# Pool groups by running sums and one difference, and attention units in four turns

## The chip, the core and the metric

The kernel runs on one core of a Trainium2 chip. The metric is device time in microseconds (us), the median of several executions of the whole kernel. Five engines work side by side, each with its own list of instructions in a fixed order: PE multiplies matrices and transposes by a multiplication with the identity, DVE does elementwise work with one or two inputs, ACT applies functions and copies, POOL does small elementwise work, and SP issues nearly all transfers. An engine takes its list strictly in order and stops at an instruction whose inputs are not there or whose output buffer is still being read.

## The reference

One decoder block over 2048 positions of 1024 values. The input is normed, projected to 2048 columns (512 for a pooling mixer and 512 each for q, k, v of 8 heads), mixed, projected back, and followed by a feed-forward part with 4096 inner columns and a squared relu.

```python
for g, w in enumerate(POOL_WINDOWS):            # 2, 4, 8, 16
    xg = ug[:, :, g, :].astype(jnp.float32)
    cs = jnp.cumsum(xg, axis=1)
    cs_lag = jnp.pad(cs, ((0, 0), (w, 0), (0, 0)))[:, :S]
    count = jnp.minimum(pos + 1, w).astype(jnp.float32)[None, :, None]
    mean = (cs - cs_lag) / count
    outs.append(mean - xg)
pooled = jnp.stack(outs, axis=2)
mapped = jnp.einsum('bsgc,gcd->bsgd', pooled, pool_w.astype(jnp.float32))
...
log1m = jnp.where(mask, jax.nn.log_sigmoid(-z), 0.0)
tail = lax.cumsum(log1m, axis=3, reverse=True) - log1m
log_a = jax.nn.log_sigmoid(z) + tail
a = jnp.where(mask, jnp.exp(log_a), 0.0)
ob = jnp.einsum('bhqk,bhkd->bhqd', a, vb.astype(jnp.float32))
```

So each of four groups of 128 pool channels takes the mean of its last 2, 4, 8 or 16 positions, less the position itself, and maps it with a 128x128 matrix. The attention weight of a key is its sigmoid times the product of one minus the sigmoids of all later keys.

## The kernel before

The 2048 positions are four tiles (j = 0 to 3) of 512. Data lies with channels on the 128 partitions and positions along the row. All large products are made of three multiplications: each fp32 operand is split into a rounded part (ACT, L145) and the rest (DVE, L146), and high times high, high times low and low times high are added up in PSUM (lines 177 to 179).

In the front part (about the first 560 us) PE runs the dense input projection, 24 multiplications of 128x512 for each block of 128 output columns (pd). Between them stand three kinds of narrow work.

- **Pool groups** (`pool_group`, one for each tile and window). ACT brings the projection from PSUM to u, 15 carried positions of the tile before stand ahead of it (POOL copies them with L390 and L395). DVE doubles the window by adding the tile to itself, shifted by 1, 2, 4, 8 (L400: one add for window 2, four for window 16), and L403 scales and subtracts u. ACT and DVE split the result (pls), and PE maps it (L410 to L412, tile pp).
- **Attention units** (`near_unit`, 64 in all: 4 tiles, 8 heads, two pairs of 128 queries each). A unit has stages, and each stage runs in a turn: first the logits on PE (pz), two sigmoids on ACT (sh, sg), a mask on POOL (L661), a running product on DVE (L663, pc) and a product that gives the weights (L672, sg); in its next turn four transposes on PE (L677, pta) and the split of the result (at); in its third turn the products with v (L689, po). `turn_stages` adds a unit and gives each unit in flight its next stage, and keeps two for the next turn. pta has two PSUM buffers, so the transposes of a unit also wait until the split of the unit before the last has read its buffer.
- **Loads** of q, k and v of a head (`near`), which SP issues while the head before is worked on.

The rest (output projection, and the feed-forward part, from about 650 us) is not touched by the change.

A scheduler puts the instructions of all engines in order when the program is built, with a timing model of its own. So an edit also moves instructions that it does not name. On the chip the lists are fixed.

Of the kernel before, what the change touches and what calls it, by code (L numbers as in the profile page):

```python
# [8 lines left out]
F32 = mybir.dt.float32  # L9
# [4 lines left out]
ALU = mybir.AluOpType  # L14

P = 128
S = 2048
D = 1024
T = 512
NT = S // T  # L20
# [8 lines left out]
WARM = 9  # L29
SCRATCH = 2048  # L30
WINDOWS = (2, 4, 8, 16)
PAD = 15
EPS = 1e-6
RATIO_FRONT = (0.3, 0.4, 0.15, 0.4, 0.4, 0.3)
RATIO_TAIL = 0.6
# [10 lines left out]
def hymba_block(ctx: ExitStack, tc: tile.TileContext, xT, gains, w_in, pool_w, w_out, w_up, w_down, out):  # L46
    nc = tc.nc
# [3 lines left out]
    const = pool("const", 1)  # L51
# [55 lines left out]
    for n in (D, D // 2):  # L107
        inv[n] = const.tile([P, 1], F32, name=f"inv{n}")
        nc.vector.memset(inv[n], 1.0 / n)
    recip = const.tile([P, PAD], F32, name="recip")  # L110
    for i in range(PAD):
        nc.vector.memset(recip[:, i:i + 1], 1.0 / (i + 1))
# [9 lines left out]
    yrlast = const.tile([P, 2, 2, TB], F32R, name="yrlast")  # L122
    carry = const.tile([P, len(WINDOWS), PAD], F32, name="carry")
    nc.vector.memset(carry, 0.0)


    qs = [[dram.tile([P, T], F32R, name=f"qs{h}_{j}") for j in range(NT)] for h in range(H)]
    ks = [[dram.tile([P, T], F32R, name=f"ks{h}_{j}") for j in range(NT)] for h in range(H)]
# [13 lines left out]
    def split(dst, src):  # L142

        hi, lo = dst
        nc.scalar.activation(hi, src, AF.Copy)  # L145
        return nc.vector.tensor_tensor(lo, src, hi.bitcast(F32), ALU.subtract)  # L146
# [147 lines left out]
    def pool_weights():  # L294
        raw = pa.tile([P, PAD + T], F32, tag="s", name="pw_raw")[:, 0:4 * P].rearrange("p (g c) -> p g c", g=4)
        nc.sync.dma_start(raw, pool_w)
        pw.append(pa.tile([P, 2, 4, P], F32R, name="pw", bufs=1))
        split((pw[0][:, 0], pw[0][:, 1]), raw)

# [85 lines left out]
    def pool_group(j, g, ps):  # L385
        w = WINDOWS[g]
        if g == 0:
            st[j]["y"] = pa.tile([P, 4, T], F32, tag="yb", name="yb", bufs=1)
        u = pa.tile([P, PAD + T], F32, tag="u", name="u")
        nc.gpsimd.tensor_copy(u[:, 0:PAD], carry[:, g])  # L390
        if j == 0:
            took = nc.vector.tensor_tensor(u[:, PAD:], ps, st[0]["r"], ALU.mult)
        else:
            took = nc.scalar.activation(u[:, PAD:], ps, AF.Copy)
        nc.gpsimd.tensor_copy(carry[:, g], u[:, T:T + PAD])  # L395
        cur, lag = u, 1
        while lag < w:
            nxt = pa.tile([P, PAD + T], F32, tag="s", name="s")
            lo = 2 * lag - 1
            nc.vector.tensor_tensor(nxt[:, lo:], cur[:, lo:], cur[:, lo - lag:PAD + T - lag], ALU.add)  # L400
            cur, lag = nxt, 2 * lag
        pl = pa.tile([P, T], F32, tag="ev", name="pl")
        nc.vector.scalar_tensor_tensor(pl, cur[:, PAD:], 1.0 / w, u[:, PAD:], op0=ALU.mult, op1=ALU.subtract)  # L403
        if j == 0:
            nc.vector.tensor_tensor(pl[:, 0:w - 1], cur[:, PAD:PAD + w - 1], recip[:, 0:w - 1], ALU.mult)
            nc.vector.tensor_tensor(pl[:, 0:w - 1], pl[:, 0:w - 1], u[:, PAD:PAD + w - 1], ALU.subtract)
        d = pa.tile([P, 2, T], F32R, tag="st", name="pls", align_bytes=256, bufs=3)
        split((d[:, 0], d[:, 1]), pl)
        pp = psx.tile([P, T], F32, tag="px", name="pp")
        nc.tensor.matmul(pp, pw[0][:, 0, g], d[:, 0], start=True, stop=False)  # L410
        nc.tensor.matmul(pp, pw[0][:, 0, g], d[:, 1], start=False, stop=False)
        nc.tensor.matmul(pp, pw[0][:, 1, g], d[:, 0], start=False, stop=True)  # L412
        nc.scalar.activation(st[j]["y"][:, g], pp, AF.Copy, scale=gs[:, g:g + 1])
        return took
# [83 lines left out]
    def attend(j, h2):  # L498
        begun[j] = begun.get(j, 0) + 1
        end = begun[j] == H // 2  # L500
        note(lambda: todo.extend([near(j, h2)] + [near_end(j)] * end))
# [131 lines left out]
    def sigmoids(pz):  # L633
        n = pz.shape[-1]
        sh = att.tile([P, T], F32, tag="sh", name="sh")
        nc.scalar.activation(sh[:, T - n:], pz, AF.Sigmoid, scale=-0.125)
        sg = att.tile([P, T], F32, tag="sg", name="sg", bufs=3)
        nc.scalar.activation(sg[:, T - n:], pz, AF.Sigmoid, scale=0.125)
        return sh, sg

# [9 lines left out]
    def near_unit(j, h, p, t):  # L650


        c0 = P if j == 0 and p == 0 else 0
        pz = psz.tile([P, T], F32, tag="pz", name="pz")
        pc = att.tile([P, T + 4], F32, tag="pc", name="pc")
        for i in range(2):
            b, lo = 2 * p + i, c0 if i == 0 else 0
            logits(pz[:, i * 256 + lo:(i + 1) * 256], t["qa"], t["qb"], b, t["kw"][:, b * P + lo:(b + 2) * P], i == 0, i == 1)
        sh, sg = sigmoids(pz[:, c0:])
        own = sg.rearrange("p (i n) -> p i n", i=2)[:, :, P:]  # L660
        nc.gpsimd.affine_select(out=own, in_=own, pattern=[[0, 2], [-1, P]], base=0,  # L661
                                channel_multiplier=1, compare_op=ALU.is_gt, fill=0.0)
        nc.vector.tensor_tensor_scan(pc[:, c0:T][:, ::-1], sh[:, c0:][:, ::-1], later_keys[:, c0:][:, ::-1], 1.0,  # L663
                                     op0=ALU.mult, op1=ALU.max)

        if c0:
            for lo, hi in ((c0, 255), (256, 511)):
                nc.vector.tensor_tensor(sg[:, lo:hi], sg[:, lo:hi], pc[:, lo + 1:hi + 1], ALU.mult)
        else:
            sg2 = sg.rearrange("p (i n) -> p i n", i=2)  # L670
            pc2 = pc[:, 0:T].rearrange("p (i n) -> p i n", i=2)
            nc.vector.tensor_tensor(sg2[:, :, 0:255], sg2[:, :, 0:255], pc2[:, :, 1:256], ALU.mult)  # L672
            nc.gpsimd.tensor_copy(left[j][:, 2 * p:2 * p + 2, h], pc2[:, :, 0])
        yield
        pt = pst.tile([P, T], F32, tag="pt", name="pta")
        for x in range(c0 // P, TB):
            nc.tensor.transpose(pt[:, x * P:(x + 1) * P], sg[:, x * P:(x + 1) * P], ident)  # L677
        at = att.tile([P, 2, T], F32R, tag="at", name="at")
        split((at[:, 0, c0:], at[:, 1, c0:]), pt[:, c0:])
        yield  # L680
        if p == 0:
            t["po"] = pso.tile([P, T], F32, tag="po", name="po")
        po, vw = t["po"], t["vw"]
        both, own, prev = (P, 3 * P, 1, 0), (3 * P, T, 2, P), (0, P, 0, 0)
        av = [(both, 0), (own, 0), (own, 1), (both, 1)] + ([] if c0 else [(prev, 0), (prev, 1)])

        for n, ((lo, hi, v, to), x) in enumerate(av):
            m = DH if x else P
            nc.tensor.matmul(po[0:m, p * 256 + to:p * 256 + to + hi - lo], vw[:, 2 * p + v, 0:m], at[:, x, lo:hi],  # L689
                             start=(p == 0 and n == 0), skip_group_check=True, stop=(p == 1 and n == len(av) - 1))  # L690
        if p == 1:
            if h % 2 == 0:
                t["ot"] = ots[j, h // 2] = att.tile([P, T], F32, tag="ot", name="ot", bufs=1)
            halves_sum(ots[j, h // 2], po, h % 2)
            if h % 2:
                nc.sync.dma_start(os_[j][h // 2], ots.pop((j, h // 2)))
        yield

    ots, stages = {}, []

    def turn_stages():

        for unit in stages:
            next(unit)
        del stages[:len(stages) - 2]

    def near(j, h2):
        def load(h):
            t = {}
            t["qa"], t["qb"] = load_q(j, h)  # L710
            t["kw"] = kw = att.tile([P, P + T], F32R, tag="k", name="kw")
            t["vw"] = vw = att.tile([P, TB + 1, P], F32R, tag="vv", name="vw")
            if j > 0:
                nc.sync.dma_start(kw[:, 0:P].bitcast(F32), ks[h][j - 1][:, T - P:].bitcast(F32))
                nc.sync.dma_start(vw[:, 0].bitcast(F32), vs[h][j - 1][:, T - P:].bitcast(F32))
            nc.sync.dma_start(kw[:, P:].bitcast(F32), ks[h][j].bitcast(F32))
            nc.sync.dma_start(vw[:, 1:].rearrange("p b d -> p (b d)").bitcast(F32), vs[h][j].bitcast(F32))
            return t

        t = load(2 * h2)  # L720
        for e in range(2):
            for p in range(2):
                stages.append(near_unit(j, 2 * h2 + e, p, t))
                turn_stages()
                if p == 0:
                    t2 = load(2 * h2 + 1) if e == 0 else None
                yield 0.27
            t = t2
# [865 lines left out]
    pa = inner.enter_context(tc.tile_pool(name="pa", bufs=2))  # L1594
# [70 lines left out]
```

## Time and profile before

| what | value |
|---|---|
| median of 3 runs | 1904.27 us (1900.44 to 1905.4) |
| the profiled execution, its time and its span | 1902.05 us, 1900.3 us |
| PE busy in the span | 1868.9 us (98%) |
| DVE busy | 1481.2 us (78%) |
| ACT busy | 1025.2 us (54%) |
| PE idle from 50 to 600 us | 10.65 us (550.00 less 539.35) |

How to read it: PE's multiplications overlap, one of 128x512 is listed with 390 ns although the next starts after 226 ns (200 us for 884 of them), so a busy PE need not be at its full rate, and PE's idle time and the granted clock (PEclk) show where time is lost. A row of the waits names the waiting engine and line, what it waited for, and then the us in total, the times, and the longest. A row of the timeline has the start, the time taken, engine, line, operation and tiles, and in brackets the idle time before it and what ended it.

### The profile page before, as it was taken

The numbers are of one execution on the slowest core, as the hardware profiler recorded it, in microseconds if no ns is written. First come the engines' busy times: TensorE is split into PE (matmuls) and PEld (weight loads), VectorE is DVE, ScalarE is ACT, GpSimd is POOL, SyncE is SP. The second block draws the span as 40 slices with busy tenths as digits, with TensorE's granted clock in tenths as the row PEclk, the third lists the DMA queues.
The fourth block names the chain that finished last, engine by engine and source line by source line (L and its number), as shares of the span: only waits on it lengthen the run. The fifth ranks groups of instructions, "written<-read, shape, count | busy, mean of one in ns | idle before, by whom it ended". The sixth has DMA issues, their size and how long they took to land.

```text
span 1900.3 us, 26640 instructions
## 1 busy us (share of the span) xinstructions
PE 1868.9 (98%) x8883; PEld 1554.3 (82%) x8883; DVE 1481.2 (78%) x2151; ACT 1025.2 (54%) x1616; POOL 238.5 (13%) x463
## 2 busy tenths in 40 slices
PE   9999999999999999999999999999999999999997
PEld 7788788788888888777888888887888888888886
DVE  6887789678866886778799988786666677988774
ACT  6565567455644465554567555554332665656543
POOL 0233234122321050000000000000010010020120
PEclk9999999999999999999999999999999999999998
DMA  7676596699888777787899888889999899999852
GB/s 226 212 255 201 177 313 224 194 322 315 281 310 312 278 252 254 284 303 274 307 358 328 303 308 281 298 284 333 388 313 330 281 317 307 332 294 341 289 206 91
DMA packets 222164, 535.91 MB, mean 282 GB/s; under 512 B 26048, under 2 KB 32192, under 8 KB 218176
## 3 DMA queue, kind: packets, MB, share of 16 engines
q1 hardware_dynamic: 217264, 525.46, 79.4%
q0 software_dynamic: 4608, 8.39, 2.4%
q8 instruction: 72, 1.18, 0.3%
q14 instruction: 76, 0.62, 0.1%
q10 hardware_dynamic: 144, 0.26, 0.0%
HBM read 349.46 MB, written 184.55 MB: 281 GB/s over the span
## 4 chain that ended last, share of the span: by engine, by line
PE 50%; DMA 5%; DVE 2%; issue 1%; ACT 1%; POOL 0%; SPq 0%; DVEq 0%; ACTq 0%
PE pb L1291 14%; PE pY L1118 13%; PE pb L1468 12%; PE pZ L1118 7%; PE pX L1118 3%; DMA ar<-sd 1%; DMA hn<-hs 1%; DMA ar<-sdi 1%; PE pb L1408 1%; DMA td<-t 0%; DMA t<-in_w_down_dram 0%; DMA b<-in_w_down_dram 0%; DMA wr<-in_w_down_dram 0%; DVE ad L146 0%; DVE hw L146 0%
## 5 line engine op out<-in xcount | busy, mean ns | idle before, releaser
L1118 PE MATMUL pY<-sa,hw 128*128 128x512 f32 x1536 | 366.3, 390 | 1.9 <-ACT u L1041 1.9
L1118 PEld LDWEIGHTS pY<-sa,hw 128*128 128x128 f32 x1536 | 287.9, 188 | 63.0 <-ACT u L1041 3.4
L1291 PE MATMUL pb<-ad,wd 128*128 128x512 f32 x1344 | 305.4, 389 | 0.7 <-DVE ad L146 0.7
L177 PE MATMUL pd<-h,hl 128*128 128x512 f32 x752 | 297.9, 396 | 1.5 <-DVE qk L146 1.3
L178 PE MATMUL pd<-h,hl 128*128 128x512 f32 x752 | 297.0, 395 | 0.3 <-DVE h L146 0.3
L179 PE MATMUL pd<-h,hl 128*128 128x512 f32 x752 | 297.3, 395 | 0.0
L1291 PEld LDWEIGHTS pb<-ad,wd 128*128 128x128 f32 x1344 | 252.1, 188 | 53.8 <-DVE ad L146 1.5
L1468 PE MATMUL pb<-ad,wd 128*128 128x512 f32 x1104 | 253.9, 390 | 0.9 <-ACT ad L145 0.9
L1468 PEld LDWEIGHTS pb<-ad,wd 128*128 128x128 f32 x1104 | 206.5, 188 | 44.6 <-ACT ad L145 1.3
L146 DVE TENSOR_TENSOR ad<-ar,ad 128x1024 fp32r<-128x1024 f32 x160 | 194.1, 1221 | 44.1 <-ACT ad L145 43.5
L145 ACT ACTIVATE ad<-ar 128x1024 fp32r<-128x1024 f32 x160 | 168.4, 1054 | 95.7 <-PE pb L1468 31.9
L1118 PE MATMUL pZ<-sa,hw 128*128 128x512 f32 x768 | 186.8, 390 | 1.7 <-DVE a L1061 1.7
L1118 PEld LDWEIGHTS pZ<-sa,hw 128*128 128x128 f32 x768 | 143.9, 188 | 32.7 <-DVE a L1061 3.0
L145 ACT ACTIVATE hl<-raw 128x512 fp32r<-128x512 f32 x168 | 104.1, 629 | 115.6 <-PE pd L179 76.7
L177 PEld LDWEIGHTS pd<-h,hl 128*128 128x128 f32 x752 | 142.2, 189 | 29.0 <-DVE qk L146 1.8
L179 PEld LDWEIGHTS pd<-h,hl 128*128 128x128 f32 x752 | 142.0, 189 | 28.2 <-DVE hl L146 0.5
L178 PEld LDWEIGHTS pd<-h,hl 128*128 128x128 f32 x752 | 142.2, 189 | 27.1 <-DVE h L146 0.7
L146 DVE TENSOR_TENSOR hl<-raw,hl 128x512 fp32r<-128x512 f32 x168 | 115.1, 690 | 46.9 <-ACT hl L145 46.5
L1035 ACT ACTIVATE a<-a 128x512 f32<-128x512 f32 x96 | 60.1, 629 | 89.6 <-DVE a L1077 38.5
L146 DVE TENSOR_TENSOR hw<-rt,hw 128x512 fp32r<-128x512 f32 x128 | 86.5, 686 | 25.2 <-ACT hw L145 25.1
L145 ACT ACTIVATE wd<-wq 128x1024 fp32r<-128x1024 f32 x56 | 59.4, 1060 | 77.1 <-PE pb L1291 68.4
L146 DVE TENSOR_TENSOR wd<-wq,wd 128x1024 fp32r<-128x1024 f32 x56 | 68.5, 1222 | 34.3 <-ACT wd L145 32.8
(218 smaller groups left out, 2737.3 us busy)
## 6 DMA issues: line engine op xcount, KB each, us to landing
ar<-sd SPq DMA_DIRECT2D x96, 512.0 KB, 5.9
ar<-sdi SPq DMA_DIRECT2D x64, 512.0 KB, 5.6
rb<-in_w_up_dram SPq DMA_DIRECT2D x30, 1024.0 KB, 6.2
sd<-a SPq DMA_DIRECT2D x104, 256.0 KB, 5.2
raw<-in_w_in_dram SPq DMA_DIRECT2D x50, 512.0 KB, 4.6
sdi<-hr SPq DMA_DIRECT2D x96, 256.0 KB, 5.4
wr<-in_w_down_dram SPq DMA_DIRECT2D x48, 512.0 KB, 5.7
sd<-s SPq DMA_DIRECT2D x88, 256.0 KB, 4.9
```

The costliest lines, as they stand in the source:

```text
L145: nc.scalar.activation(hi, src, AF.Copy)
L146: return nc.vector.tensor_tensor(lo, src, hi.bitcast(F32), ALU.subtract)
L177: nc.tensor.matmul(ps, hl[:, 0, c], hi, start=(k == 0), stop=False)
L178: nc.tensor.matmul(ps, hl[:, 0, c], lo, start=False, stop=False)
L179: last_mm[0] = nc.tensor.matmul(ps, hl[:, 1, c], hi, start=False, stop=(k == n - 1))
L1035: nc.scalar.activation(t, src, AF.Relu)
L1118: nc.tensor.matmul(t, w[:, wx, c], a[:, ax, c % 2], start=first and c == 0 and x == 0, stop=last and c == G - 1 and x == 2, skip_group_che ...
L1291: nc.tensor.matmul(b, t[:, wx, 2 * (kk % 2) + c, i * P:(i + 1) * P], a[:, ax, c], start=p in ("P1", "P5", "P2") and kk == 0 and c == 0 and ...
L1408: nc.tensor.matmul(b[:, cols], block(t, wx, c, n), a[:, ax, c, cols], start=False, stop=(i == 1 and c == 1 and x == 2), skip_group_check=True)
L1468: nc.tensor.matmul(ps[q, n], block(t, wx, c, n), left_[q][:, ax, c], start=(n_ in ("P1", "P3") and kk == 0 and c == 0 and x == 0), stop=(n ...
```

## The change

Pool groups. For window 2 one subtraction is left: the position before less the position itself, and the factor one half is put into the pool matrix of that group when it is loaded (a multiplication of 128x128 at the start). Window 4 keeps its two adds and the scaled subtraction. For windows 8 and 16 one running sum takes the place of the three or four adds: at each position it adds u and subtracts u of w positions before, starting from a kept sum. The kept sum of the last w positions is made by a reduction, for all tiles but the last. 16 positions are carried in place of 15.

Attention units. A unit now rests for one turn between making its weights and transposing them, so four units are in flight (three are kept for the next turn), and the weights sg have four buffers, not three. The loads of v move from the place where the head's q and k are loaded, one head ahead, to the head's own first turn, behind that turn's work.

```diff
--- before.py
+++ after.py
@@ -29,7 +29,7 @@
 WARM = 9
 SCRATCH = 2048
 WINDOWS = (2, 4, 8, 16)
-PAD = 15
+PAD = 16
 EPS = 1e-6
 RATIO_FRONT = (0.3, 0.4, 0.15, 0.4, 0.4, 0.3)
 RATIO_TAIL = 0.6
@@ -122,6 +122,8 @@
     yrlast = const.tile([P, 2, 2, TB], F32R, name="yrlast")
     carry = const.tile([P, len(WINDOWS), PAD], F32, name="carry")
     nc.vector.memset(carry, 0.0)
+    window_sum = const.tile([P, len(WINDOWS)], F32, name="window_sum")
+    nc.vector.memset(window_sum, 0.0)
 
 
     qs = [[dram.tile([P, T], F32R, name=f"qs{h}_{j}") for j in range(NT)] for h in range(H)]
@@ -294,6 +296,7 @@
     def pool_weights():
         raw = pa.tile([P, PAD + T], F32, tag="s", name="pw_raw")[:, 0:4 * P].rearrange("p (g c) -> p g c", g=4)
         nc.sync.dma_start(raw, pool_w)
+        nc.vector.tensor_scalar(raw[:, 0], raw[:, 0], 1.0 / WINDOWS[0], None, op0=ALU.mult)
         pw.append(pa.tile([P, 2, 4, P], F32R, name="pw", bufs=1))
         split((pw[0][:, 0], pw[0][:, 1]), raw)
 
@@ -393,17 +396,26 @@
         else:
             took = nc.scalar.activation(u[:, PAD:], ps, AF.Copy)
         nc.gpsimd.tensor_copy(carry[:, g], u[:, T:T + PAD])
-        cur, lag = u, 1
-        while lag < w:
-            nxt = pa.tile([P, PAD + T], F32, tag="s", name="s")
-            lo = 2 * lag - 1
-            nc.vector.tensor_tensor(nxt[:, lo:], cur[:, lo:], cur[:, lo - lag:PAD + T - lag], ALU.add)
-            cur, lag = nxt, 2 * lag
         pl = pa.tile([P, T], F32, tag="ev", name="pl")
-        nc.vector.scalar_tensor_tensor(pl, cur[:, PAD:], 1.0 / w, u[:, PAD:], op0=ALU.mult, op1=ALU.subtract)
-        if j == 0:
-            nc.vector.tensor_tensor(pl[:, 0:w - 1], cur[:, PAD:PAD + w - 1], recip[:, 0:w - 1], ALU.mult)
-            nc.vector.tensor_tensor(pl[:, 0:w - 1], pl[:, 0:w - 1], u[:, PAD:PAD + w - 1], ALU.subtract)
+        if w == 2:
+            nc.vector.tensor_tensor(pl, u[:, PAD - 1:PAD + T - 1], u[:, PAD:], ALU.subtract)
+            if j == 0:
+                nc.vector.tensor_tensor(pl[:, 0:1], u[:, PAD:PAD + 1], u[:, PAD:PAD + 1], ALU.subtract)
+        else:
+            sums = pa.tile([P, PAD + T], F32, tag="s", name="s")
+            if w == 4:
+                pair = pa.tile([P, PAD + T], F32, tag="s", name="s")
+                nc.vector.tensor_tensor(pair[:, PAD - 2:], u[:, PAD - 2:], u[:, PAD - 3:PAD + T - 1], ALU.add)
+                nc.vector.tensor_tensor(sums[:, PAD:], pair[:, PAD:], pair[:, PAD - 2:PAD + T - 2], ALU.add)
+            else:
+                nc.vector.tensor_tensor_scan(sums[:, PAD:], u[:, PAD:], u[:, PAD - w:PAD + T - w], window_sum[:, g:g + 1],
+                                             op0=ALU.add, op1=ALU.subtract)
+                if j < NT - 1:
+                    nc.vector.tensor_reduce(window_sum[:, g:g + 1], u[:, PAD + T - w:], axis=mybir.AxisListType.X, op=ALU.add)
+            nc.vector.scalar_tensor_tensor(pl, sums[:, PAD:], 1.0 / w, u[:, PAD:], op0=ALU.mult, op1=ALU.subtract)
+            if j == 0:
+                nc.vector.tensor_tensor(pl[:, 0:w - 1], sums[:, PAD:PAD + w - 1], recip[:, 0:w - 1], ALU.mult)
+                nc.vector.tensor_tensor(pl[:, 0:w - 1], pl[:, 0:w - 1], u[:, PAD:PAD + w - 1], ALU.subtract)
         d = pa.tile([P, 2, T], F32R, tag="st", name="pls", align_bytes=256, bufs=3)
         split((d[:, 0], d[:, 1]), pl)
         pp = psx.tile([P, T], F32, tag="px", name="pp")
@@ -634,7 +646,7 @@
         n = pz.shape[-1]
         sh = att.tile([P, T], F32, tag="sh", name="sh")
         nc.scalar.activation(sh[:, T - n:], pz, AF.Sigmoid, scale=-0.125)
-        sg = att.tile([P, T], F32, tag="sg", name="sg", bufs=3)
+        sg = att.tile([P, T], F32, tag="sg", name="sg", bufs=4)
         nc.scalar.activation(sg[:, T - n:], pz, AF.Sigmoid, scale=0.125)
         return sh, sg
 
@@ -672,6 +684,7 @@
             nc.vector.tensor_tensor(sg2[:, :, 0:255], sg2[:, :, 0:255], pc2[:, :, 1:256], ALU.mult)
             nc.gpsimd.tensor_copy(left[j][:, 2 * p:2 * p + 2, h], pc2[:, :, 0])
         yield
+        yield
         pt = pst.tile([P, T], F32, tag="pt", name="pta")
         for x in range(c0 // P, TB):
             nc.tensor.transpose(pt[:, x * P:(x + 1) * P], sg[:, x * P:(x + 1) * P], ident)
@@ -702,20 +715,23 @@
 
         for unit in stages:
             next(unit)
-        del stages[:len(stages) - 2]
+        del stages[:max(0, len(stages) - 3)]
 
     def near(j, h2):
         def load(h):
             t = {}
             t["qa"], t["qb"] = load_q(j, h)
             t["kw"] = kw = att.tile([P, P + T], F32R, tag="k", name="kw")
+            if j > 0:
+                nc.sync.dma_start(kw[:, 0:P].bitcast(F32), ks[h][j - 1][:, T - P:].bitcast(F32))
+            nc.sync.dma_start(kw[:, P:].bitcast(F32), ks[h][j].bitcast(F32))
+            return t
+
+        def load_v(h, t):
             t["vw"] = vw = att.tile([P, TB + 1, P], F32R, tag="vv", name="vw")
             if j > 0:
-                nc.sync.dma_start(kw[:, 0:P].bitcast(F32), ks[h][j - 1][:, T - P:].bitcast(F32))
                 nc.sync.dma_start(vw[:, 0].bitcast(F32), vs[h][j - 1][:, T - P:].bitcast(F32))
-            nc.sync.dma_start(kw[:, P:].bitcast(F32), ks[h][j].bitcast(F32))
             nc.sync.dma_start(vw[:, 1:].rearrange("p b d -> p (b d)").bitcast(F32), vs[h][j].bitcast(F32))
-            return t
 
         t = load(2 * h2)
         for e in range(2):
@@ -723,6 +739,7 @@
                 stages.append(near_unit(j, 2 * h2 + e, p, t))
                 turn_stages()
                 if p == 0:
+                    load_v(2 * h2 + e, t)
                     t2 = load(2 * h2 + 1) if e == 0 else None
                 yield 0.27
             t = t2
```

What the scheduler makes of it, at two places. In the changed program the lines below line 126 have moved: the split's L146 is L148 there, the running product's L663 is L675, the weights' product L672 is L684, the transposes' L677 are L690, and the products with v, L689, are L702.

The first place is DVE's list at tile 1, window 16. Before, from its third add on (L400; L403 ends the group, and pls is the split that PE's second mapping product needs):

```order
L400 TENSOR_TENSOR s<-s 128x520
L146 TENSOR_TENSOR hl<-raw,hl 128x512
L663 SCALAR_TENSOR_TENSOR pc<-sh,later_keys 128x512
L648 TENSOR_TENSOR ot<-ot,po 64x512
L400 TENSOR_TENSOR s<-s 128x512
L672 TENSOR_TENSOR sg<-sg,pc 128x2x255
L740 TENSOR_SCALAR zero<-left_137 128x16
L146 TENSOR_TENSOR at<-pta,at 128x384
L146 TENSOR_TENSOR hl<-raw,hl 128x512
L403 SCALAR_TENSOR_TENSOR pl<-s,u 128x512
L741 TENSOR_REDUCE zall<-zero 128x1
L146 TENSOR_TENSOR pls<-pl,pls 128x512
```

Now, from the running sum on (L411, which the list names by its general form), L414 is the reduction, L415 the scaled subtraction:

```order
L411 SCALAR_TENSOR_TENSOR s<-u,window_sum 128x512
L148 TENSOR_TENSOR hl<-raw,hl 128x512
L278 SCALAR_TENSOR_TENSOR nt<-xt,gains,r_2321 128x512 x2
L675 SCALAR_TENSOR_TENSOR pc<-sh,later_keys 128x384
L414 TENSOR_REDUCE window_sum<-u 128x1
L415 SCALAR_TENSOR_TENSOR pl<-s,u 128x512
L148 TENSOR_TENSOR h<-nt,h 128x512
L148 TENSOR_TENSOR at<-pta,at 128x384
L148 TENSOR_TENSOR h<-nt,h 128x512
L680 TENSOR_TENSOR sg<-sg,pc 128x127
L680 TENSOR_TENSOR sg<-sg,pc 128x255
```

Before, the group's rows from the first add (15 rows above this piece) to L403 were 26 instructions in all, now they are 7, from L411 to L415; the split pls follows L415 as the eighth instruction, where it was the second.

The second place is PE's list at the last units of tile 2, with buffer numbers: the weights of the logits pz with number n are sg with number n + 8. Before:

```order
L677 MATMUL pta_4338<-ident_98,sg_4288 128x128 x4
L179 MATMUL pd_4318<-h_4188,hl_4100 128x512
L630 MATMUL pz_4402<-kw_4236,qa_4231 128x256
L631 MATMUL pz_4402<-kw_4236,qb_4232 128x256
L630 MATMUL pz_4402<-kw_4236,qa_4231 128x256
L631 MATMUL pz_4402<-kw_4236,qb_4232 128x256
L677 MATMUL pta_4394<-ident_98,sg_4354 128x128 x4
L689 MATMUL po_4331<-at_4277,vw_4197 128x256
L689 MATMUL po_4331<-at_4277,vw_4197 128x128
L689 MATMUL po_4331<-at_4277,vw_4197 64x128
L689 MATMUL po_4331<-at_4277,vw_4197 64x256
```

Now, the same stretch of the work:

```order
L642 MATMUL pz_4301<-kw_4194,qa_4189 128x256
L643 MATMUL pz_4301<-kw_4194,qb_4190 128x256
L642 MATMUL pz_4301<-kw_4194,qa_4189 128x256
L690 MATMUL pta_4293<-ident_98,sg_4180 128x128 x2
L422 MATMUL pp_4137<-pls_4134,pw_660 128x512
L690 MATMUL pta_4293<-ident_98,sg_4180 128x128 x2
L643 MATMUL pz_4301<-kw_4194,qb_4190 128x256
L702 MATMUL po_4218<-at_4169,vw_4021 128x256
```

Before, the unit of pz_4402 is followed at once by the transposes of the unit just ahead of it (sg_4354, of pz_4346), six rows behind the transposes of the one before that. Now the transposes beside the logits pz_4301 are of sg_4180: the unit in between (pz_4233, sg_4241) is transposed a turn later.

## The prediction

> **What bounds the kernel now.** I read the page first, for the engines' shares.
>
> ```profile
> PE 1868.9 (98%) x8883; PEld 1554.3 (82%) x8883; DVE 1481.2 (78%) x2151; ACT 1025.2 (54%) x1616; POOL 238.5 (13%) x463
> ```
>
> PE is busy nearly throughout, and the change leaves its 8883 multiplications as they are. So the change can only win back time in which PE stood or ran at a lower clock. Second came the table of stretches, whose columns are busy time by engine, then PEclk, DMA share and GB/s: a steady stretch of the feed-forward part, the sum from 50 to 600 us, and the two stretches of 25 us where PE lost most, each with a closer look.
>
> ```profile
> 1000.00:1200.00 200.00, 200.00 (x884) 165.64 (x883) 175.59 (x280) 114.62 (x200) 0.00 (x0) 1.00 0.87 302
> ...
> 200.00:225.00 25.00, 20.79 (x102) 16.97 (x101) 20.09 (x35) 13.35 (x24) 5.22 (x4) 0.93 0.57 164
> 300.00:325.00 25.00, 25.00 (x142) 21.37 (x141) 24.60 (x38) 17.98 (x35) 13.87 (x14) 1.00 0.62 200
> 325.00:350.00 25.00, 22.16 (x111) 18.10 (x111) 23.29 (x35) 14.06 (x26) 8.05 (x10) 0.86 0.57 186
> sum 550.00, PE 539.35 PEld 456.37 DVE 442.45 ACT 313.50 POOL 153.08; mean PE 24.52 PEld 20.74 DVE 20.11 ACT 14.25 POOL 6.96
> ...
> 335.00:340.00 5.00, 3.13 (x22) 2.56 (x21) 5.00 (x9) 3.03 (x5) 1.52 (x2) 1.00 0.32 108
> 340.00:345.00 5.00, 4.33 (x21) 3.71 (x22) 4.94 (x9) 3.87 (x8) 0.60 (x2) 0.55 0.42 147
> ```
>
> 884 multiplications in 200 us are one each 0.226 us, at full clock: from 650 us on, outside the change, nothing is to be had. From 50 to 600 us PE idles 550.00 - 539.35 = 10.65 us. Place A (200 to 225) loses 4.21 us idle and 25 x 0.07 = 1.75 us of clock, 5.96 in all. Place B (325 to 350) loses 2.84 and 25 x 0.14 = 3.5, so 6.34. All that PE loses here is then 10.65 + 5.25 = 15.9 us, and A and B are 12.3 of it. Third, the waits of PE name who is late.
>
> ```profile
> PE pp L410 <- ACT pls L145: 4.0, 1, 4.0
> PE pta L677 <- DVE at L146: 1.9, 1, 1.9
> PE pd L177 <- DVE qk L146: 1.3, 2, 0.8
> PE po L689 <- DVE at L146: 0.7, 1, 0.7
> PE po L689 <- DVE ot L648: 0.7, 1, 0.7
> ```
>
> Every one is a wait for DVE or for ACT behind DVE. The timeline tells why. Place A is the pool group of tile 1 with window 16:
>
> ```profile
> 191.82 0.60 ACT L394 ACTIVATE u<-pd 128x512 f32<-128x512 f32 x1 [0.72 <-PE pd L179]
> 193.65 0.69 DVE L400 TENSOR_TENSOR s<-u 128x526 f32<-128x526 f32 x1
> ...
> 206.44 0.67 DVE L400 TENSOR_TENSOR s<-s 128x512 f32<-128x512 f32 x1
> ...
> 208.95 0.68 DVE L403 SCALAR_TENSOR_TENSOR pl<-s,u 128x512 f32<-128x512 f32 x1
> 209.66 0.63 ACT L145 ACTIVATE pls<-pl 128x512 fp32r<-128x512 f32 x1 [2.63 <-DVE pl L403]
> 210.35 0.50 PE L410 MATMUL pp<-pls,pw 128*128 128x512 f32 x1 [3.98 <-ACT pls L145]
> ```
>
> DVE needs 16.0 us (193.65 to 209.63) for the 26 instructions of its list from the first add to L403; the four adds alone are spread over 12.8. At place B four transposes wait for a PSUM buffer, whose split stands behind a running product, the last pool add and a product, on a DVE that has no free moment (5.00 of 5.00):
>
> ```profile
> 331.61 0.60 PE L677 MATMUL pta<-ident,sg 128*128 128x128 f32 x4
> 336.82 1.21 DVE L663 TENSOR_TENSOR_SCAN pc<-sh,later_keys 128x512 f32<-128x512 f32 x1
> 337.95 0.65 DVE L400 TENSOR_TENSOR s<-s 128x512 f32<-128x512 f32 x1
> 338.54 0.67 DVE L672 TENSOR_TENSOR sg<-sg,pc 128x510 f32<-128x510 f32 x1
> 339.14 0.67 DVE L146 TENSOR_TENSOR at<-pta,at 128x512 fp32r<-128x512 f32 x1
> 339.87 0.66 PE L677 MATMUL pta<-ident,sg 128*128 128x128 f32 x4 [1.87 <-DVE at L146]
> ```
>
> **The change part by part.** First, DVE's work.
>
> ```profile
> L663 DVE TENSOR_TENSOR_SCAN pc<-sh,later_keys 128x512 f32<-128x512 f32 x56 | 68.6, 1226 | 0.7 <-ACT sh L636 0.7
> L400 DVE TENSOR_TENSOR s<-u 128x526 f32<-128x526 f32 x16 | 11.2, 697 | 3.6 <-ACT u L394 3.6
> L403 DVE SCALAR_TENSOR_TENSOR pl<-s,u 128x512 f32<-128x512 f32 x16 | 10.8, 677 | 0.0
> L400 DVE TENSOR_TENSOR s<-s 128x524 f32<-128x524 f32 x12 | 8.3, 692 | 0.1
> L400 DVE TENSOR_TENSOR s<-s 128x520 f32<-128x520 f32 x8 | 5.5, 693 | 0.1
> L400 DVE TENSOR_TENSOR s<-s 128x512 f32<-128x512 f32 x4 | 2.7, 670 | 0.0
> L741 DVE TENSOR_REDUCE zall<-zero 128x1 f32<-128x32 f32 x3 | 0.5, 178 | 0.0
> ```
>
> Out go 40 adds and 16 subtractions, 11.2 + 8.3 + 5.5 + 2.7 + 10.8 = 38.5 us. In come 12 adds or differences and 12 scaled subtractions at 0.68 (16.3), 8 running sums, 6 reductions at 0.18 (1.1) and some 0.3 for the pool matrix at the start, hidden because PE wants that matrix only with the first group's mapping, behind the projection of seven blocks. A running sum that adds and subtracts is not in this trace: between an add (0.68) and twice the running product (2.45), I take the running product's 1.23, the nearest row, so 9.8. The balance is -11 us (bounds -15 and -1). As a total it is worth nothing, since DVE has 22% free; it counts only where DVE is late.
>
> Place A. Before, 51 wide and 29 narrow multiplications stand between the group's projection and L410; 51 x 0.226 is 11.5, and PE took 14.5 us, from 191.82, where ACT took up the projection, to 210.35 - 3.98 = 206.37, where it fell idle; so a narrow one takes 0.1. In the changed list it is 38 wide and 19 narrow, 8.6 + 1.9 = 10.5 us: PE comes 4 us earlier. DVE's piece has 7 instructions: running sum 1.2, split 0.6, two scalings 1.5, a running product 0.9, reduction 0.2, scaled subtraction 0.7, together 5.1 us in place of 16.0. From 193.65 that ends at 198.8, ACT's split by about 200, and PE comes at 191.8 + 10.5 = 202.3. The second mapping product needs DVE's split, 8 rows and about 4.9 us later, at 203.7, and stands some 2.9 us behind the first, at 205.2. The margins are 2.3 and 1.5 us, and a running sum of 2.45 would eat half. I count 5.7 of 5.96 us as won.
>
> Place B. Back to back DVE starts a row every 0.60 us (338.54, 339.14, 339.74). Pricing the rows so, and each DVE row by the PE rows it stands beside in the two lists, the two stretches of 25 PE-us before B hold an estimated 24.7 and 18.2 us of DVE work before, 22.8 and 13.1 now (at A 25.2, now 20.7). Between two uses of a transpose buffer, PE has 4.8 us of work at B, the closest pair in this part of the program; the matching pair now has 6.4, with a split that lies 6 DVE rows behind, not 7 with the add among them. I count 5.3 of 6.34.
>
> The pause. The weights (sg) now stand a median of 5 us of PE work ahead of their transposes in the list, before 1.4. No row shows PE waiting for sg alone, so this wins nothing by itself, but it frees the scheduler to put DVE's splits earlier. Price: the split must still come before the products with v. Counting PE work against DVE rows as above, seven units now have PE up to 1.5 us ahead of the split, against three before; for units before, this count fell about 1 us short of the slack in the trace. I add +1.5 us (bounds 0, and B's 6.3 for any place that passes 1.9 us).
>
> The loads. SP issues v later.
>
> ```profile
> vw<-vs SPq DMA_DIRECT2D x32, 256.0 KB, 4.3
> ```
>
> It lands in 4.3 us; the shortest lead in PE work between issue and use is 8 us now, 6.6 before, and what queues behind on SP (weights, next q and k) is no longer held by a v buffer that only the next turn frees. Zero, unless the lead falls below 4.3. The other waits (10.65 - 4.21 - 2.84 = 3.6 us of idle time) are reshuffled: zero, bounds -3.6 and +3.6.
>
> Sum: -5.7 - 5.3 + 1.5 = -9.5. The profiled execution took 1902.05 us, so 1892.5. It lies 2.2 below the median of the runs shown (1904.27), off which the sum would give 1894.8; I say 1893.5.
>
> Here a rule can be weighed. At B, 1.87 us of idle time and 0.67 right after it were followed by a granted clock of 0.55 over 5 us. The Trainium skill ("TensorE: Matmul & The Clock Gate", section "Why this matters for your kernels") says that the clock falls after idle gaps of more than about 3 us between bursts. By it B would have lost no clock, the gain would be 3.5 smaller and the time 1896; the trace disagrees, and the measurement decides.
>
> **The rivals.** (1) One stall of B's kind stays or comes up elsewhere: DVE is still nearly full before B (24.60 of 25). The gain shrinks by 6.3: 1899.8. (2) The stalls only move, as the scheduler fills each stretch anew and tight rows return: 1902 to 1905. Against it: fewer DVE rows at both places. (3) Slower: with four units in flight PE reaches products with v before DVE's split, at several of the seven units. From 1.9 us on, such a wait also costs clock and is priced as B, 6.3. With four of them against the two now, 1902 + 2 x 6.3 = 1914.7. For it: the seven counts; against: each is at most 1.5.
>
> **How the numbers follow.** Forecast 0.58 (1888 to 1898), rival 1 0.22, rival 2 0.11, rival 3 0.09. A measurement of this kernel can tell about 0.3%, or 5.7 us, from no change: faster is below 1898.6. The forecast and two fifths of rival 1 are faster, 0.66; slower is rival 3, 0.09; the rest, 0.25, the same. The range starts at 1885, about where all 15.9 us are won (1886.2), and goes to 1904, which leaves out rival 3 and part of rival 2.
>
> **What would show it.** The running sums take about 1.23 us; the pool mapping no longer waits at tile 1; PE idles under 6 us from 50 to 600, with PEclk 1.00 throughout. The prediction is wrong if a clock below 0.9 appears in a stretch of 25 us there, or if products with v wait on DVE for 2 us or more.

## The result, and the profile after

| what | before | after |
|---|---|---|
| median, us | 1902.41 (1900.44 to 1905.4, 4 runs) | 1887.41 (1885.92 to 1888.39, 4 runs) |
| profiled execution, its time and its span, us | 1902.05, 1900.3 | 1888.39, 1886.4 |
| PE idle from 50 to 600 us | 10.65 us | 2.73 us |
| clock lost there, in the 25-us stretches | 5.25 us | 0 |

Before are the three runs shown ahead of the prediction and a fourth.
The ratio of after to before is 0.9917, with a 95% interval from 0.9904 to 0.9929: faster by 0.83%, 15.0 us between the medians.

The page of after first, with its row of engines, and then its table of stretches (busy time by engine, PEclk, DMA share, GB/s) at the two places of the prediction, with the stretch before the second and the sum from 50 to 600 us:

```profile
PE 1862.2 (99%) x8883; PEld 1550.0 (82%) x8883; DVE 1470.3 (78%) x2135; ACT 1024.9 (54%) x1616; POOL 227.8 (12%) x463
...
200.00:225.00 25.00, 25.00 (x136) 21.39 (x135) 19.16 (x33) 13.60 (x25) 5.99 (x19) 1.00 0.81 251
...
300.00:325.00 25.00, 23.79 (x132) 19.76 (x131) 24.60 (x36) 17.45 (x34) 12.42 (x17) 1.00 0.64 207
325.00:350.00 25.00, 25.00 (x132) 21.13 (x133) 17.13 (x26) 9.40 (x17) 4.83 (x19) 1.00 0.75 228
...
sum 550.00, PE 547.27 PEld 465.56 DVE 442.44 ACT 319.30 POOL 149.56; mean PE 24.88 PEld 21.16 DVE 20.11 ACT 14.51 POOL 6.80
```

Both places are full and at full clock. PE's idle time fell by 7.92 us (547.27 less 539.35) and the lost clock by 5.25, together 13.2 us. The span became 13.9 us shorter, so nearly all of the gain lies in this part of the program. Beside place B a little is left, 1.21 us from 300 to 325, where DVE is as full as before (24.60 of 25).

The waits of PE from 20 to 620 us (us in total, times, longest), all that are listed above 0.3:

```profile
PE pd L179 <- DVE qk L148: 1.1, 2, 0.8
PE po L702 <- DVE ot L660: 0.7, 1, 0.7
PE pta L690 <- DVE at L148: 0.5, 1, 0.5
PE pta L690 <- DVE sg L684: 0.4, 1, 0.4
```

The wait of the pool mapping (pp, 4.0 before) is gone, that of the transposes for a buffer went from 1.9 to 0.5, and no product with v waits for its split (po on at).

The timeline at place A, tile 1 with window 16, from the running sum to the mapping:

```profile
189.76 1.27 DVE L411 TENSOR_TENSOR_SCAN s<-u,window_sum 128x512 f32<-128x512 f32 x1
...
193.96 0.68 DVE L415 SCALAR_TENSOR_TENSOR pl<-s,u 128x512 f32<-128x512 f32 x1
194.67 0.63 ACT L147 ACTIVATE pls<-pl 128x512 fp32r<-128x512 f32 x1 [0.51 <-DVE pl L415]
...
197.96 0.68 DVE L148 TENSOR_TENSOR pls<-pl,pls 128x512 fp32r<-128x512 f32 x1
...
198.47 0.48 PE L422 MATMUL pp<-pls,pw 128*128 128x512 f32 x1
...
201.54 0.40 PE L423 MATMUL pp<-pls,pw 128*128 128x512 f32 x1
```

From the first row of the group to the end of the scaled subtraction DVE takes 4.88 us (189.76 to 194.64), where it took 16.0. ACT is done at 195.30, PE comes 3.2 us later; DVE's split is done at 198.64, and the product that needs it comes 2.9 us later. No row of PE has a bracket: nothing was waited for.

The groups of DVE's instructions (count, busy us, mean ns):

```profile
L411 DVE TENSOR_TENSOR_SCAN s<-u,window_sum 128x512 f32<-128x512 f32 x8 | 10.4, 1297 | 0.2 <-ACT u L397 0.2
L415 DVE SCALAR_TENSOR_TENSOR pl<-s,u 128x512 f32<-128x512 f32 x12 | 8.2, 687 | 0.0
L401 DVE TENSOR_TENSOR pl<-u 128x512 f32<-128x512 f32 x4 | 2.7, 675 | 0.9 <-ACT u L397 0.9
L414 DVE TENSOR_REDUCE window_sum<-u 128x1 f32<-128x16 f32 x3 | 0.5, 154 | 0.0
```

A running sum takes 1.30 us, and DVE works 10.9 us less in all (1481.2 to 1470.3).

### The profile page after: what moved, and what is told of

Same layout as the page of the kernel before. It is cut to its first block, busy times and chain, and to the rows that moved or that the text cites. A ratio compares the mean times of both kernels' runs of the same rounds, so it can differ in the third digit from the quotient of the medians.

```text
span 1886.4 us, 26655 instructions
## 1 busy us (share of the span) xinstructions
PE 1862.2 (99%) x8883; PEld 1550.0 (82%) x8883; DVE 1470.3 (78%) x2135; ACT 1024.9 (54%) x1616; POOL 227.8 (12%) x463
## 4 chain that ended last, share of the span: by engine, by line
PE 48%; DMA 6%; DVE 3%; issue 1%; ACT 1%; POOL 0%; SPq 0%; DVEq 0%; ACTq 0%
PE pb L1308 14%; PE pY L1135 12%; PE pb L1485 12%; PE pZ L1135 6%; PE pX L1135 3%; DMA ar<-sd 1%; DMA ar<-sdi 1%; DMA hn<-hs 1%; PE pb L1425 1%; DMA b<-in_w_down_dram 1%; DVE hw L148 0%; DMA td<-t 0%; DMA sdi<-a 0%; DMA t<-in_w_down_dram 0%; DMA rb<-in_w_up_dram 0%
## 5 line engine op out<-in xcount | busy, mean ns | idle before, releaser
L148 DVE TENSOR_TENSOR ad<-ar,ad 128x1024 fp32r<-128x1024 f32 x160 | 194.0, 1220 | 42.8 <-ACT ad L147 42.4
L148 DVE TENSOR_TENSOR hl<-raw,hl 128x512 fp32r<-128x512 f32 x168 | 114.9, 689 | 50.5 <-ACT hl L147 49.2
L148 DVE TENSOR_TENSOR hw<-rt,hw 128x512 fp32r<-128x512 f32 x128 | 86.4, 684 | 24.4 <-ACT hw L147 24.3
L148 DVE TENSOR_TENSOR wd<-wq,wd 128x1024 fp32r<-128x1024 f32 x56 | 68.4, 1222 | 35.6 <-ACT wd L147 34.1
```

## The experiments

Four kernels ran on one chip and four on another, each against the kernel before on the same chip (its median was 1903.98 us on the first, 1903.6 on the second). In the diffs `-` and `+` are against the kernel named. Line numbers shift by some lines between kernels: pp is always the mapping of the pool group, pls its split, s its sums, pta the transposes, at their split. "Lost" is PE's idle time from 50 to 600 us plus the clock lost in the stretches of 25 us.

| kernel | ratio to before, 95% interval | lost, us |
|---|---|---|
| before | 1 | 10.65 + 5.25 |
| after | 0.9917 [0.9904, 0.9929] | 2.73 + 0 |
| pool groups alone | 0.9918 [0.9887, 0.9949] | 2.12 + 0 |
| turns and loads alone | 0.9984 [0.9968, 1.0] | 10.15 + 5.25 |
| after, loads of v at their old place | 0.9925 [0.9901, 0.995] | 2.14 + 0 |
| before, loads of v later | 0.9995 [0.9984, 1.0005] | 11.39 + 1.75 |
| before, running sum for window 16 alone | 0.9944 [0.9926, 0.9962] | 3.52 + 0 |
| before, new forms for all but window 16 | 0.9958 [0.9942, 0.9974] | 7.55 + 1.75 |
| after, one more add per pool group | 0.9919 [0.99, 0.9937] | 6.73 + 0 |
| after, a second turn of rest | 0.9925 [0.9907, 0.9943] | 4.21 + 1.75 |

### Which part of the change it is

**The pool groups alone.** The kernel before with the change's pool groups; near_unit, turn_stages and near stay:

```diff
-        sg = att.tile([P, T], F32, tag="sg", name="sg", bufs=4)
+        sg = att.tile([P, T], F32, tag="sg", name="sg", bufs=3)
...
-        del stages[:max(0, len(stages) - 3)]
+        del stages[:len(stages) - 2]
```

(against after, with the second `yield` and the moved loads taken back too).

> The pool groups as in the change, the attention units and the loads of v as before. Theory D (DVE's list was late at two places, and the pool groups' long chains of adds made it so): the first place, 5.96 us, goes fully, because the chain of the group with window 16 is short now; at the second place the last pool add goes out from ahead of the split, and the list gives the transposes' buffer an estimated 2 us or more of margin, where it had 0.9, so 4 to 6.3 us go there. About 10 to 12 us faster than before, ratio 0.9937 to 0.9947. Rival S (any edit makes the scheduler fill the lists anew, and the two stalls were an accident of one filling; the parts by themselves mean nothing): the time of a part has nothing to do with what it takes out; stalls of 2 us or more turn up at other places, and the parts' gains do not add up. Rival P (the pause did it): within 3 us of before.

Measured: 1889.9 us, 0.9918. The stretch from 50 to 600 us, and its largest wait:

```profile
50.00:600.00 550.00, 547.88 (x2990) 465.04 (x2990) 444.04 (x681) 318.87 (x580) 145.44 (x335) 1.00 0.80 268
```

```profile
PE pd L179 <- DVE qk L148: 0.7, 1, 0.7
```

All of the gain is there, place B's too, without any pause. The gain is larger than the expected 10 to 12 us, but the interval takes in the expected ratios.

**The turns and loads alone.** Four units in flight, four buffers for sg, later loads of v; pool groups as before:

```diff
-        sg = att.tile([P, T], F32, tag="sg", name="sg", bufs=3)
+        sg = att.tile([P, T], F32, tag="sg", name="sg", bufs=4)
...
         yield
+        yield
...
-        del stages[:len(stages) - 2]
+        del stages[:max(0, len(stages) - 3)]
```

> The attention units in four turns, with four buffers of weights and the later loads of v, the pool groups as before. Theory D: the first place stays (a wait of the pool mapping for ACT behind DVE of 3 to 4 us, with a lower clock behind it), because the 26 rows of DVE's list from the first add to the scaled subtraction are hardly fewer; at the second place the transposes' buffer gains margin (2.2 us by the list, was 0.9), but the pool mapping there has none still. So 3 to 6 us faster, ratio 0.9968 to 0.9984, with the 4 us wait at 200 to 225 us still in the trace. Rival S: no such pattern. Rival P: nearly the whole 14 us, ratio 0.993 or lower.

Measured: 0.9984, at the edge of the expected band and on the edge of no difference. The waits and the two stretches:

```profile
PE pp L410 <- ACT pls L145: 4.9, 2, 3.0
PE pd L177 <- DVE qk L146: 2.2, 2, 1.2
```

```profile
200.00:225.00 25.00, 22.31 (x108) 18.18 (x107) 20.32 (x34) 14.82 (x27) 2.80 (x5) 0.93 0.64 193
325.00:350.00 25.00, 21.61 (x103) 17.20 (x101) 20.88 (x31) 12.26 (x22) 7.06 (x8) 0.86 0.54 165
```

The rest did what it can do: the transposes no longer wait at B. But PE then stood at the next thing that comes out of DVE's list, the mapping of window 16 of the next tile: now both waits are for the pool groups (2.0 us at A, less than the 3 to 4 expected, and 3.0 at B), and both stretches still lose clock. One execution of ten took 4979.67 us and is left out of the ratio. The program has a branch at its end that computes the attention and what follows anew; whether this execution went through it no trace shows, and the cause stays open.

**The loads.** Once the change with v loaded where it was before, once the kernel before with v loaded later:

```diff
             if j > 0:
                 nc.sync.dma_start(kw[:, 0:P].bitcast(F32), ks[h][j - 1][:, T - P:].bitcast(F32))
+                nc.sync.dma_start(vw[:, 0].bitcast(F32), vs[h][j - 1][:, T - P:].bitcast(F32))
             nc.sync.dma_start(kw[:, P:].bitcast(F32), ks[h][j].bitcast(F32))
+            nc.sync.dma_start(vw[:, 1:].rearrange("p b d -> p (b d)").bitcast(F32), vs[h][j].bitcast(F32))
...
-                    load_v(2 * h2 + e, t)
```

> The changed kernel with the loads of v at their old place, one head ahead. The lists of PE, DVE, ACT and POOL are then those of the change; only SP's differs. Theory D: the same as the change, ratio 0.991 to 0.993. Rival V (the later loads of v matter, since a load of v that waits for its buffer holds SP's list with the weights and the next q and k behind it): 2 us or more slower than the change, with waits of PE behind transfers.

> The kernel before with the later loads of v alone; the lists of PE, DVE, ACT and POOL stay as before. Theory D: the same as before within 2 us, both stalls in place. Rival V: 2 us or more faster, or, if v now comes late for a unit that needs it two turns later, slower with PE waiting at the products with v behind a transfer.

Measured: 0.9925 and 0.9995. The kernel before keeps its order on PE, DVE, ACT and POOL exactly. The change keeps it on DVE and POOL, and on PE and ACT but for four small moves between 405 and 453 us. The times are the same: the place of the loads is worth nothing that these runs can tell.

### Chain or load: why the pool groups do it

The pool part takes 10.9 us of work from DVE and, at the same time, makes the chain from projection to mapping shorter. Two kernels share that work out, 5.3 and 5.5 us as reckoned from the rows (DVE's whole busy time fell by 4.6 and 4.2), and one gives it back.

**Window 16 alone.** In the kernel before, the adds stay for windows 2, 4 and 8:

```diff
+            if w < 16:
+                cur, lag = u, 1
+                while lag < w:
...
+            else:
...
+                    nc.vector.tensor_tensor_scan(sums[:, PAD:], u[:, PAD:], u[:, PAD - w:PAD + T - w], window_sum[:, g:g + 1],
+                                                 op0=ALU.add, op1=ALU.subtract)
```

> The kernel before, with the running sum for window 16 alone; windows 2, 4 and 8 and the attention units are as before. It saves DVE 4 x (2.75 - 1.30) less three reductions of 0.15, about 5.3 us. Theory C (the chain of four adds of window 16, shared out over DVE's list, is what came late at both places): no wait of the pool mapping above 1 us, PE idle from 50 to 600 us under 4.5 us, ratio to the kernel before 0.991 to 0.994. Theory W (DVE's work as a whole is what counts, half of it is saved): about half of the gain, ratio 0.995 to 0.997, a wait of 1 to 3 us left at one of the two places.

Measured: 0.9944, between the bands of the two theories. The stretch from 50 to 600 us, then the one from 640 to 700, and the wait there:

```profile
50.00:600.00 550.00, 546.48 (x2986) 464.44 (x2985) 448.31 (x691) 321.09 (x581) 146.39 (x331) 1.00 0.80 268
640.00:700.00 60.00, 57.45 (x258) 47.42 (x257) 46.86 (x66) 34.45 (x52) 25.24 (x29) 0.97 0.75 257
```

```profile
PE pd L179 <- DVE acc L846: 2.5, 1, 2.5
```

Half of the saved work brought nearly the whole gain in the front part (3.52 us lost, of 15.9). What the time lacks lies in a new wait at 659 us, 2.55 us and 60 x 0.03 = 1.8 of clock, behind the front part, where PE waits for an addition on DVE. Why DVE is late there stays open. Without these 4.35 us the ratio would be 0.992; that each execution has them is assumed from one trace.

**All but window 16.** In the kernel before, the adds stay for window 16:

```diff
+        if w == 2:
+            nc.vector.tensor_tensor(pl, u[:, PAD - 1:PAD + T - 1], u[:, PAD:], ALU.subtract)
...
+            if w == 16:
+                cur, lag = u, 1
+                while lag < w:
...
+                    nc.vector.tensor_tensor_scan(sums[:, PAD:], u[:, PAD:], u[:, PAD - w:PAD + T - w], window_sum[:, g:g + 1],
+                                                 op0=ALU.add, op1=ALU.subtract)
```

> The kernel before, with the new forms for windows 2, 4 and 8, while window 16 keeps its four adds; the attention units are as before. It saves DVE 4 x 0.70 for window 2 and 4 x 0.78 less 0.46 for window 8, about 5.5 us, as much as the running sum of window 16 alone. Theory C: the pool mapping of window 16 still waits 3 to 4 us at tile 1 (200 to 225 us), with or without a loss of clock, and there is a wait left near 335 us; PE idle from 50 to 600 us is 7 to 10 us, ratio 0.997 to 1.000. Theory W: half of the gain, ratio 0.995 to 0.997, with the same waits as the kernel with window 16 alone.

Measured: 0.9958, in theory W's band, and its interval overlaps that of window 16 alone, so the two times don't decide. The trace does, where theory W expected the same waits in both kernels: the waits of the mapping, the stretch of place A, and the group there:

```profile
PE pp L431 <- DVE pls L148: 3.1, 2, 1.8
PE pp L430 <- ACT pls L147: 1.2, 1, 1.2
```

```profile
200.00:225.00 25.00, 21.94 (x106) 17.75 (x105) 20.11 (x34) 12.82 (x24) 4.42 (x5) 0.93 0.58 177
```

```profile
193.49 0.70 DVE L410 TENSOR_TENSOR s<-u 128x526 f32<-128x526 f32 x1
...
205.65 0.68 DVE L423 SCALAR_TENSOR_TENSOR pl<-s,u 128x512 f32<-128x512 f32 x1
206.74 0.61 ACT L147 ACTIVATE pls<-pl 128x512 fp32r<-128x512 f32 x1
207.41 0.50 PE L430 MATMUL pp<-pls,pw 128*128 128x512 f32 x1 [1.24 <-ACT pls L147]
208.99 0.68 DVE L148 TENSOR_TENSOR pls<-pl,pls 128x512 fp32r<-128x512 f32 x1
209.72 0.50 PE L431 MATMUL pp<-pls,pw 128*128 128x512 f32 x1 [1.81 <-DVE pls L148]
```

As much work saved, and place A stays: the four adds and the scaled subtraction are still spread over 12.8 us (193.49 to 206.33), and PE loses 3.06 us and 1.75 of clock, 4.8 of the 5.96. So at A it is the chain. At B it is not window 16's chain alone: the transposes wait for their buffer there in neither kernel, so either half of the change frees them, and this kernel did better than theory C said. A wait of 1.3 us of the mapping is left at 337 us.

One rival of the expectations is left, that the two stalls were an accident of one filling of the lists and any new filling would do. At A it does not hold: in all six kernels with the running sum for window 16 the stretch from 200 to 225 is full (25.00), and in all four without it PE idles 2.7 to 4.2 us there, whatever else was changed. At B it is weaker: from 325 to 350 the seven kernels with any of the new forms idle at most 1.3 us, the three without them 2.8 to 3.4, and one of the seven, with the second rest, still loses 1.75 us of clock. Small waits do move with each filling.

**The work given back.** The change with one add more per pool group, written behind the group's split, read by nobody:

```diff
         split((d[:, 0], d[:, 1]), pl)
+        extra = pa.tile([P, T], F32, tag="dum", name="extra", bufs=1)
+        nc.vector.tensor_tensor(extra, u[:, PAD:], u[:, PAD:], ALU.add)
```

> The changed kernel with one more add of 128x512 on DVE for each pool group, whose result nobody reads, written behind the group's split. It puts 16 x 0.68 = 10.9 us of DVE work back, as much as the change took away, but outside the chain from the projection to the mapping. Theory C: as the change, ratio 0.990 to 0.994, PE idle from 50 to 600 us under 4.5 us. Theory W: the gain is gone, ratio 0.998 to 1.001.

Measured: 0.9919. The added group, the front part, and the group at place A:

```profile
L422 DVE TENSOR_TENSOR extra<-u 128x512 f32<-128x512 f32 x16 | 11.0, 685 | 0.0
```

```profile
50.00:600.00 550.00, 543.27 (x2963) 460.60 (x2963) 449.18 (x694) 319.19 (x579) 147.36 (x321) 1.00 0.80 267
```

```profile
193.38 1.27 DVE L411 TENSOR_TENSOR_SCAN s<-u,window_sum 128x512 f32<-128x512 f32 x1
194.57 0.67 DVE L422 TENSOR_TENSOR extra<-u 128x512 f32<-128x512 f32 x1
...
198.60 0.68 DVE L415 SCALAR_TENSOR_TENSOR pl<-s,u 128x512 f32<-128x512 f32 x1
```

DVE has its 11.0 us back and the gain stays, so theory W falls. The add did not stay outside the chain everywhere: at A the scheduler put it behind the running sum, and the group takes 5.9 us (193.38 to 199.28) in place of 4.88. That is still far from 16.0, and PE waits for nothing there. It is not worth nothing either: the trace loses 6.73 us and not under 4.5, in small waits of at most 1.7 us, none of which costs clock.

**A second rest.** The change with five units in flight:

```diff
-        sg = att.tile([P, T], F32, tag="sg", name="sg", bufs=4)
+        sg = att.tile([P, T], F32, tag="sg", name="sg", bufs=5)
...
         yield
+        yield
...
-        del stages[:max(0, len(stages) - 3)]
+        del stages[:max(0, len(stages) - 4)]
```

> The changed kernel with a second turn of rest before the transposes: five units in flight, five buffers for the weights. If the rest is worth nothing (what the pool part alone showed): ratio to the kernel before 0.990 to 0.994, as the change. If a rest does help, by giving DVE more time: below 0.990, PE idle from 50 to 600 us under 2 us. If units in flight cost (rival 3 of the prediction): products with v wait for DVE's split by 2 us or more at some units, ratio over 0.995.

Measured: 0.9925. In time, more rest neither helps nor costs; rival 3's mechanism, products with v ahead of the split, has no wait in the trace even here.

## Why the prediction was right, point by point

The direction, the places and the mechanism held; the size was a third too small: 9.5 us forecast, 13.7 between the two profiled executions, 15.0 between the medians. 1887.41 lies in the range, outside the forecast's own band by 0.6 us.

| term of the sum | predicted, us | measured between the two traces, us |
|---|---|---|
| place A, 200 to 225 | -5.7 | -5.96 |
| place B, 325 to 350, with what came up at 300 to 325 | -5.3 | -6.34 + 1.21 = -5.13 |
| products with v ahead of DVE's split | +1.5 | 0 |
| other waits from 50 to 600 | 0 | (2.73 - 1.21) - 3.6 = -2.1 |
| sum | -9.5 | -13.2 |

- **Place A** was right in its working: PE's margins over ACT and DVE were given as 2.3 and 1.5 us, they are 3.2 and 2.9. All the signs that it named are there, the clock of 1.00 among them. The running sum was costed at the running product's 1.23 us and took 1.30. Of the two things that the pool part does at once, less DVE work and a shorter chain for window 16, the shorter chain is shown to be needed: with only the other windows shortened, A stays.
- **Place B** came out to 0.2 us. The reason was in part a different one. The prediction credited fewer DVE rows and the longer distance between two uses of a transpose buffer, which comes of the rest; the pool groups alone won B without the rest, and the rest alone only handed the stall on to the mapping. So that the size came out so closely is in part luck.
- **The step that failed** is the pause's price, "I add +1.5 us". It took a count of PE's work against DVE's rows, in which seven units were tight, for a wait, although the same count had fallen about 1 us short for units before. The trace has no such wait, nor has that of the second rest. Measured, the price is 0.
- **The other waits** "are reshuffled: zero" was the second mis-sized term. They fell by 2.1 us. DVE's 10.9 us were called worth nothing as a total; with that work put back, these small waits grew by 4.0 us (2.73 to 6.73) in the one trace there is. That suggests that DVE's free time holds off small waits, and that a zero with bounds on both sides should have leaned to the side of less work. It is not shown: PE idles 2.1 to 4.2 us in the four kernels with all of the new forms and no added work, and the times (0.9919 against 0.9917) do not tell.
- **The loads** at zero were right. **Rival 2** (the stalls only move) is what the turns alone would have been, and none of the products with v that **rival 3** feared waited.
- **The clock.** The prediction took B's 3.5 us of clock as lost by every execution. With the kernel before and only v loaded later, B idles the same 1.87 us, and the stretch keeps its clock:

```profile
325.00:350.00 25.00, 21.79 (x120) 17.36 (x119) 23.90 (x36) 14.68 (x27) 8.40 (x11) 1.00 0.60 198
```

Its span was 1897.1 us, 3.2 below the profiled span of before, though the medians are alike: the execution profiled was the fastest of its ten. So part of the sum, 3.5 us, seems to be a loss that comes in some executions and not in others. That is read from two traces of two kernels; it fits that the mean granted clock of 35 executions of before on the two chips of the experiments runs from 0.993 to 0.997. Nor is the 1.9 us from which on a wait was to cost clock a bound: 1.87 us did not cost it here, and 1.80 us did at another place, shown at the end.

## What to carry to other kernels

When an in-order engine of some 80% load makes another wait, look at the chain that is spread over its list before its total: each link of a chain waits behind all that the order put in between, so four adds and a scaled subtraction of 0.7 us each took 16 us, and one running sum of 1.3 us with the same subtraction took 5. Giving the waiting side more time elsewhere, by one more unit in flight, here only handed the stall to the next consumer of the same engine. And a wait that was counted on paper and has no row in the trace of before is worth its price only if the count agrees with the trace for the waits that are there.

## What the runs showed of the hardware

In these traces the clock falls by a fixed grid, not by the length of a gap. The traces record when the granted clock changes. Every drop goes to 0.50, and in the seven traces with more than one drop each begins a whole number of steps of 3.413 us after the first. In the kernel before they begin at 210.812, 340.519 and 1890.17, that is 38.0 and 492.0 steps after the first. A drop amid the program lasts one step or two, 3.41 or 6.83 us; the one at its end runs past the last instruction. Cut along that grid, the table of stretches shows what decides. The kernel before, at A and at B:

```profile
207.40:210.81 3.41, 0.46 (x1) 0.19 (x1) 2.71 (x7) 1.15 (x3) 0.56 (x2) 1.00 0.54 207
210.81:214.22 3.41, 3.19 (x8) 2.47 (x8) 3.41 (x7) 2.70 (x5) 0.00 (x0) 0.50 0.62 142
214.22:217.64 3.42, 3.42 (x16) 2.83 (x15) 1.82 (x3) 0.63 (x1) 0.00 (x0) 1.00 0.72 167
337.11:340.52 3.41, 1.54 (x11) 1.04 (x9) 3.38 (x6) 1.53 (x4) 1.17 (x1) 1.00 0.64 216
340.52:343.93 3.41, 2.75 (x15) 2.65 (x15) 3.38 (x6) 3.36 (x7) 0.60 (x2) 0.50 0.37 133
343.93:347.35 3.42, 3.42 (x9) 2.65 (x9) 3.42 (x6) 1.54 (x3) 0.19 (x1) 0.50 0.71 169
```

The kernel before with later loads of v, at B, and the end of its gap in the timeline:

```profile
336.95:340.36 3.41, 1.65 (x14) 1.38 (x12) 3.41 (x6) 2.02 (x4) 1.17 (x1) 1.00 0.46 144
340.36:343.77 3.41, 2.27 (x18) 1.72 (x18) 3.35 (x7) 2.73 (x6) 0.28 (x2) 1.00 0.57 204
```

```profile
340.47 0.66 PE L677 MATMUL pta<-ident,sg 128*128 128x128 f32 x4 [1.87 <-DVE at L146]
```

The change with v loaded at its old place, at a gap of 1.80 us in the feed-forward part:

```profile
1284.26:1287.67 3.41, 1.61 (x7) 1.02 (x6) 3.41 (x5) 1.63 (x3) 0.00 (x0) 1.00 0.48 183
1287.67:1291.08 3.41, 3.41 (x9) 2.62 (x8) 1.93 (x4) 1.26 (x2) 0.00 (x0) 0.50 0.20 77
```

A step in which PE was busy for 1.61 us or less of 3.41 is followed by a step at half clock, one with 1.65 is not. Cut so from 12 to 1868 us, all ten traces agree, but for one step: eight steps at full clock had 1.61 us or less and were followed by 0.50, and of all the others only one was, with 2.52 us busy, in the kernel with the second rest. A step that already runs at half clock seems to need more: with 2.75 us busy (340.52 above) and 2.69 (the turns alone) a second one at half clock followed, with 3.19 and more it did not. The same gap of 1.87 us lay wholly inside one step in the first kernel and was cut by its edge in the second. So in these traces about 1.8 us of idle time within one step cost half a step more, 1.7 us, or twice that as at B, and a gap of the same length across an edge cost nothing more. That is a pattern over these traces, not tested by a run of its own, and the step with 2.52 us shows that busy time is not the whole of it. The Trainium skill ("TensorE: Matmul & The Clock Gate", section "What's actually happening") says that the activity is watched in a free-running window of 3413 ns; these traces agree with that, and not with the gap of about 3 us that the prediction weighed.
